# Layer 1's mixer weights split into two parts during layer 0's MLP, kept in device memory and reloaded through a ring of five places

## The chip, the cores and the metric

The kernel runs on one core of one Trainium2 chip. The metric is the device time of one execution in microseconds (us), median of several runs. The core's engines are named as the profile names them: PE (matrix products; PEld is its loading of the stationary operand), DVE (vector), ACT (scalar), POOL (GpSimd) and SP (which here only issues transfers). A transfer (DMA) is issued by an engine's queue; SP's and POOL's are used here.

## The reference

Two layers over a residual stream x of 1024 tokens x 1024 channels, in float32. Cut to what matters:

```python
for layer in range(2):
    h = rms_norm(x, norm_mix[layer])
    if layer % 2 == 0:
        y_mix, xq = rglru_group(h, w_in_a, ...)      # recurrent block
    else:
        y_mix, xq = fox_group(h, w_in_b, ...)        # forgetting attention, 8 heads of 64
    y_mem = memory_group(xq, mem, ..., w_mem_kv[layer], ...)   # cross-attention into 256 memory tokens
    x = x + concatenate([y_mix, y_mem]) @ w_out[layer]
    x = x + square(relu(rms_norm(x, norm_mlp[layer]) @ w_mlp_in[layer])) @ w_mlp_out[layer]
```

In layer 1 (fox_group) one projection `h @ w_in_b` gives queries, keys, values, forget logits and the memory queries; `memory_group` needs `rms_norm(mem) @ w_mem_kv[1]`.

## The kernel before, in words

**Split products.** Every large product is made from three matmuls. A float32 operand is split into a high part (`hi`, rounded to the format `float32r`) and a low part (`lo`, what is left), and the product is hi·hi + hi·lo + lo·hi (`t3`, line 394). For a weight tile, ACT copies the raw tile into `wh` and DVE (or POOL) subtracts that from the raw tile into `wl` (`_wpart`, L320 and L321). For a data tile ACT writes `r` (L501) and DVE the second `r` (L504), in `split_sb`.

**The plan of weights.** `run` first appends every weight tile that will be used, in order of use, to `self.plan`; `share` then decides, entry by entry, where its data comes from. A weight tile is 128 partitions x 1024 numbers (512 KB). Raw tiles are loaded by SP's queue into four raw buffers `wr0` to `wr3` (L316) and split into a ring of three places; a place is one pair `wh`, `wl`. `wnext` and `wpair` hand out the next one or two entries and call `_wsplit`, which prepares entries up to three ahead: an entry is prepared as soon as the place of the entry three before it is free. Layer 1's mixer uses several weights twice, once for each half (h = 0 and h = 1) of the tokens: on the first use the parts are split and also stored to device memory (`wsp`, L344, SP's queue), on the second they are loaded from there (entries `"ld"`, L336, POOL's queue). `TUNE["pb0"]` and its kin say which quarters of a split POOL does in place of DVE.

**Stages**, by time in the profile: layer 0's mixer up to about 315 us; layer 0's MLP up to 949 us; layer 1's keys and values of the memory (`kv`) from 949 to 972 us; then the memory queries (`xq_proj`), `fox_proj` of h = 0, `fox` (attention) woven with the output projection and with `fox_proj` of h = 1; layer 1's MLP from about 1535 us. In `kv`, `xq_proj` and `fox_proj` two weight entries are taken at a time (`wpair`): `kv` runs 2 token tiles through a pair, 24 matmuls of 256 columns each, the others run 4.

**Layer 0's MLP** has eight groups g; each has a first half `mlp_z` (products "b11", "b21", "t2", "t3", "t1", "t4", "b22" with w_mlp_in) and a second half `mlp_out` (the same seven names with w_mlp_out), 24 matmuls of 512 columns in each product. Seven split weights come from four raw tiles by additions on DVE (`_wunit`, L359 to L364). The second half's results are added to x in device memory by accumulating transfers (`send`, L1223, POOL's queue; `xspill` is x).

**Slots.** All working tiles of 128 x 512 share a pool of 86 places (`Slots`), named `f` (float32) or `r` (float32r). The place that was given back longest ago is taken next; its next writer waits until the last reader, a transfer perhaps, is done with it.

**What sets the order.** Each engine and each queue runs its own instructions in order. The framework orders them when the program is built, with a timeline of its own, so the order on the engines is fixed and can be read from the program.

Of the kernel before, what the change touches and what calls it, by code (L numbers as in the profile page):

```python
# [77 lines left out]
class Unit:  # L78
# [3 lines left out]
    def __init__(self, src, names, at):  # L82
        self.src, self.names, self.buf, self.dve = src, names, {}, False
# [43 lines left out]
def chain(*gs):  # L127
# [39 lines left out]
    "pa": (),  # L167
    "pb0": (1, 3),
    "pb1": (0, 1, 2, 3),
    "pb2": (3,),  # L170
    "pm0": (),
    "pm1": (1, 3),
# [3 lines left out]
class Builder:  # L176
# [4 lines left out]
    def __init__(self, ctx, tc, ins, out):  # L181
# [12 lines left out]
        self.wraw = [cst.tile([P, 1056], F32, name=f"wr{i}") for i in range(4)]  # L194
        self.ubuf = [self.wraw[3][:, i * 520:i * 520 + H + 3] for i in range(2)]
# [20 lines left out]
        self.pool_parts = TUNE["pa"]  # L216
# [11 lines left out]
        for _ in range(10):  # L228
            nc.tensor.matmul(warm[:, :P], lhsT=self.ones, rhs=self.ones, start=True, stop=True)

# [37 lines left out]

    def share(self):
        own, keep = {}, {}  # L270
        for j, e in enumerate(self.plan):
            if len(e) < 5 or e[3][0] not in ('wkb','wqb','wvb0','wvb1','wxqb','wout1m','wout1x'):
                continue
            k, full = e[3], self.ins[e[3][0]].shape[2]
            if k in own:
                if k not in keep:
                    keep[k] = [self.dr.tile([P, full], F32R, name=self.nm("wsp")) for _ in range(2)]
                self.plan[j] = (None, e[1], "ld", k, e[4])
            elif e[1] == full:
                own[k] = j  # L280
        k = ("wout1x", 3)
        keep[k] = [self.dr.tile([P, 1024], F32R, name=self.nm("wsp")) for _ in range(2)]
        self.own = {j: keep[k] for k, j in own.items() if k in keep}
        self.keep = keep
        self.raws, self.rawbuf, last = [], {}, [-1] * 4
        n, mod = 0, 3
        for j, e in enumerate(self.plan):
            if isinstance(e[2], Unit):
# [4 lines left out]
            for k, src, end in todo:  # L293
                b = n % mod
                n += 1
                self.raws.append((j, src, b, last[b]))
                last[b] = end
                if k is None:
                    self.rawbuf[j] = b
                else:  # L300
                    e[2].buf[k] = self.wraw[b][:, :1024]

    def _wbuf(self, i, bufs):
        return bufs[i % len(bufs)][:, :self.plan[i][1]]

    def _wrawbuf(self, i):
        return self.wraw[self.rawbuf[i]][:, :self.plan[i][1]] if i in self.rawbuf else None

    def _wraw(self, upto):
        while self.wrawn < len(self.raws):  # L310
            i, src, b, prev = self.raws[self.wrawn]
            if i >= upto or prev >= self.wload:
                break
            n = src.shape[1]
            for s in (slice(0, n // 2), slice(n // 2, n)) if self.wrawn == 0 else (slice(0, n),):
                self.nc.sync.dma_start(self.wraw[b][:, s], src[:, s])  # L316
# [6 lines left out]
    def _wsplit(self, upto):  # L323
        nc = self.nc
        while self.wload < min(len(self.plan), upto):
# [6 lines left out]
            hi, lo = (self._wbuf(i, b) for b in (self.whi, self.wlo))  # L332
# [15 lines left out]
    def _wunit(self, hi, lo, unit, what):  # L348
        V = self.nc.vector
        G = V if unit.dve else self.nc.gpsimd  # L350
        r = unit.buf
# [3 lines left out]
        for h in range(2):  # L355
# [3 lines left out]
            G.tensor_tensor(r["a11"][:, d], r["a11"][:, d], r["a21"][:, d], ALU.subtract)  # L359
            G.tensor_tensor(x, r["a22"][:, d], r["a11"][:, d], ALU.subtract)  # L360
# [1509 lines left out]
```

## Time and profile before

| what | value |
|---|---|
| median of 3 runs | 2077.35 us (2076.72 to 2081.33) |
| the profiled execution's own time | 2074.57 us |
| its span, first to last instruction | 2072.6 us |
| PE busy | 2045.0 us, 99% of the span |
| DVE, ACT, POOL busy | 1568.6, 1152.0, 456.8 us |
| transfers | 301.55 MB, mean 145 GB/s |

How to read the profile: "busy" is the time in which an engine ran an instruction other than one that waits, branches or issues a transfer for another engine. A row of the waits says who waited for whom, the sum in us, how often, and the longest. A row of the stages ("windows") gives, for a stretch of time, its length, then the busy time of each engine with the number of its instructions, then the granted clock of PE (1.00 is full), the mean busy share of the 16 transfer engines, and GB/s. A row of a transfer queue gives packets, MB, and the time that its packets took as a share of the 16 engines over the stretch. "Landing" is the time from the issue of a transfer to its end.

### The profile page before, as it was taken

The numbers are of one execution on the slowest core, as the hardware profiler recorded it, in microseconds if no ns is written. First come the engines' busy times: TensorE is split into PE (matmuls) and PEld (weight loads), VectorE is DVE, ScalarE is ACT, GpSimd is POOL, SyncE is SP. The second block draws the span as 40 slices with busy tenths as digits, with TensorE's granted clock in tenths as the row PEclk, the third lists the DMA queues.
The fourth block names the chain that finished last, engine by engine and source line by source line (L and its number), as shares of the span: only waits on it lengthen the run. The fifth ranks groups of instructions, "written<-read, shape, count | busy, mean of one in ns | idle before, by whom it ended". The sixth has DMA issues, their size and how long they took to land. (4 is left out here: it accounts for less than half of the span.)

```text
span 2072.6 us, 29660 instructions
## 1 busy us (share of the span) xinstructions
PE 2045.0 (99%) x10382; PEld 1707.0 (82%) x10382; DVE 1568.6 (76%) x2924; ACT 1152.0 (56%) x2172; POOL 456.8 (22%) x582
## 2 busy tenths in 40 slices
PE   9999999999999999999999999999999999999999
PEld 7998778888888888879998998777777888888887
DVE  8897699776776776788685779786886767758757
ACT  7856655554554554557554646575655445545543
POOL 1022210201202202205442423222021222022021
PEclk9999999999999999999999999999999999999999
DMA  8423361635635635638777438633355576265274
GB/s 295 150 95 118 102 208 62 132 82 112 133 82 112 133 78 116 144 112 254 254 248 266 153 111 300 212 132 127 126 117 144 136 159 122 67 138 117 68 182 122
DMA packets 122645, 301.55 MB, mean 145 GB/s; under 512 B 13760, under 2 KB 15872, under 8 KB 122496
## 3 DMA queue, kind: packets, MB, share of 16 engines
q1 hardware_dynamic: 80736, 211.50, 30.2%
q0 software_dynamic: 41760, 88.16, 22.7%
q8 instruction: 81, 1.33, 0.2%
q14 instruction: 68, 0.56, 0.1%
HBM read 190.46 MB, written 109.15 MB: 145 GB/s over the span
## 5 line engine op out<-in xcount | busy, mean ns | idle before, releaser
L1067 PE MATMUL pspt<-r,wh 128*128 128x512 f32 x1536 | 493.4, 397 | 1.8 <-ACT wh L320 1.6
L321 DVE TENSOR_TENSOR wl<-wr,wh 128x1024 fp32r<-128x1024 f32 (+2 forms) x354 | 338.5, 965 | 179.0 <-ACT wh L320 177.3
L320 ACT ACTIVATE wh<-wr 128x1024 fp32r<-128x1024 f32 (+3 forms) x403 | 303.3, 777 | 295.6 <-PE pss L1067 87.8
L1223 POOL DMA_DIRECT2D xspill<-f x232 | 203.0, 1087 | 858.9 <-DVE f L1083 821.4
L1067 PEld LDWEIGHTS pspt<-r,wh 128*128 128x128 f32 x1536 | 288.3, 188 | 73.1 <-ACT wh L320 2.4
L1067 PE MATMUL pss<-r,wh 128*128 128x512 f32 x1024 | 328.7, 396 | 0.8 <-DVE r L504 0.8
L1067 PE MATMUL pspt<-r,wl 128*128 128x512 f32 x768 | 304.5, 396 | 1.1 <-DVE wl L321 1.1
L1067 PE MATMUL pspj<-r,wh 128*128 128x512 f32 x832 | 272.8, 401 | 0.7 <-DVE r L496 0.7
L389 PE MATMUL pspj<-wh,r 128*128 128x256 f32 (+1 forms) x1280 | 244.1, 285 | 3.2 <-DMA wh<-wsp 1.4
L504 DVE TENSOR_TENSOR r<-f,r 128x512 fp32r<-128x512 f32 x282 | 188.9, 685 | 73.9 <-DMA xspill<-f 56.2
L1067 PEld LDWEIGHTS pss<-r,wh 128*128 128x128 f32 x1024 | 192.3, 188 | 48.7 <-DVE r L504 1.7
L501 ACT ACTIVATE r<-f 128x512 fp32r<-128x512 f32 x282 | 169.3, 625 | 79.5 <-DMA xspill<-f 24.7
L389 PEld LDWEIGHTS pspj<-wh,r 128*128 128x128 f32 x1280 | 201.5, 189 | 6.1 <-DMA wh<-wsp 1.9
L1067 PE MATMUL pss<-r,wl 128*128 128x512 f32 x512 | 202.5, 395 | 0.0
L1067 PEld LDWEIGHTS pspj<-r,wh 128*128 128x128 f32 x832 | 157.5, 190 | 39.2 <-DVE r L496 1.3
L389 PE MATMUL pspj<-wl,r 128*128 128x256 f32 (+1 forms) x640 | 182.3, 285 | 0.4 <-DVE wl L321 0.4
L1067 PEld LDWEIGHTS pspt<-r,wl 128*128 128x128 f32 x768 | 144.7, 188 | 36.5 <-DVE wl L321 1.5
L1067 PE MATMUL pspj<-r,wl 128*128 128x512 f32 x416 | 165.3, 398 | 0.0
L389 PE MATMUL pspj<-r,wh 128*128 128x512 f32 x480 | 157.5, 404 | 1.9 <-ACT r L493 0.5
L1088 ACT ACTIVATE f<-f 128x512 f32<-128x512 f32 x128 | 78.7, 625 | 102.9 <-DVE f L1087 100.7
L389 PEld LDWEIGHTS pspj<-wl,r 128*128 128x128 f32 x640 | 120.7, 189 | 1.6 <-DVE wl L321 0.6
L1067 PEld LDWEIGHTS pss<-r,wl 128*128 128x128 f32 x512 | 96.2, 188 | 23.5 <-issue 0.2
(302 smaller groups left out, 3564.2 us busy)
## 6 DMA issues: line engine op xcount, KB each, us to landing
wr<-in_w_dram SPq DMA_DIRECT2D x136, 512.0 KB, 4.0
xspill<-f POOLq DMA_DIRECT2D x232, 256.0 KB, 7.3
f<-xspill SPq DMA_DIRECT2D x88, 256.0 KB, 4.4
xspill<-f SPq DMA_DIRECT2D x56, 256.0 KB, 3.0
wsp<-wh SPq DMA_DIRECT2D x22, 512.0 KB, 5.9
wsp<-wl SPq DMA_DIRECT2D x22, 512.0 KB, 5.9
wh<-wsp POOLq DMA_DIRECT2D x21, 512.0 KB, 5.8
wl<-wsp POOLq DMA_DIRECT2D x21, 512.0 KB, 5.8
```

Of the source, the lines that this page charges most:

```text
L320: self.wact = self.nc.scalar.activation(hi, raw, AF.Copy)
L321: eng.tensor_tensor(lo, raw, hi.bitcast(F32), ALU.subtract)
L389: self.lastmm = self.nc.tensor.matmul(out, lhsT=a, rhs=b, start=(j == 0), stop=(j == n - 1))
L501: i = self.nc.scalar.activation(hi[:, :n], src, AF.Copy)
L504: self.nc.vector.tensor_tensor(lo[:, :n], src, hi[:, :n].bitcast(F32), ALU.subtract)
L1067: self.lastmm = self.nc.tensor.matmul(ps, lhsT=a, rhs=b, start=(start and c == 0 and j == 0), stop=(c == n - 1 and j == 2), skip_group_che ...
L1088: self.lastsq = self.nc.scalar.activation(f[:, n], f[:, n], AF.Square)
L1223: nc.gpsimd.dma_start(self.xs[2 * q + a, :, b * H:(b + 1) * H], f[:, n], accum_op=ALU.add)
```

## The change

The weights of layer 1's mixer (`LATE`, and the second half of `wkv`) are all made entries of the kind `"ld"`, first uses too. `share` lists them in `todo` as 66 pieces of up to 512 columns. During layer 0's MLP, at the start of most products from the second half of g = 0 on, `pre_tick` loads up to two pieces into slots (SP's queue, line 325 of the changed file), and three ticks later splits them with `split_sb` and stores both parts into `wsp` (POOL's queue, line 335: 132 stores of 256 KB). In the mixer all 55 uses are loads of 512 KB for each of the two parts (line 377, POOL's queue: 110 loads, where there were 46). The mixer no longer has any raw weights, so the four raw buffers become two more places: from the first `kv` entry to the last one of `fox_proj`, the ring has five. The table of POOL's quarters goes away.

The core of the diff:

```diff
+        self.wp = ctx.enter_context(tc.tile_pool(name="wp", bufs=1))
+        self.wide = [(-1, None)] * 4
...
     def share(self):
...
+            k = e[3]
+            if k[0] not in self.LATE and not (k[0] == "wkv" and k[1] >= 8):
+                continue
...
+            if k not in self.keep:
+                full = self.ins[k[0]].shape[2]
+                self.keep[k] = [self.dr.tile([P, full], F32R, name=self.nm("wsp")) for _ in range(2)]
+                n = -(-full // H)
+                self.todo += [(k, q * full // n, full // n) for q in range(n)]
+            self.plan[j] = (None, e[1], "ld", k, e[4])
+
+        rings = [(a, b) for a, b in zip(self.whi, self.wlo)]
+        wide = rings + [(0, 1), (2, 3)]
...
+            b = min(range(len(wide) if first <= j < end else len(rings)), key=lambda i: (used[i], i))
+            self.ring.append(wide[b])
+            self.prior.append(used[b])
+            used[b] = j
...
+    def pre_load(self, n):
+        for _ in range(min(n, len(self.todo))):
+            k, a, w = self.todo.pop(0)
+            f = self.F.get()
+            self.nc.sync.dma_start(f[:, :w], self.ins[k[0]][k[1]][:, a:a + w])
+            self.inload.append((self.ticks, k, a, w, f))
+
+    def pre_split(self):
+        self.ticks += 1
+        while self.inload and self.inload[0][0] <= self.ticks - 3:
+            _, k, a, w, f = self.inload.pop(0)
+            parts = self.split_sb(f[:, :w], w)
+            self.F.put(f)
+            for r, d in zip(parts, self.keep[k]):
+                self.nc.gpsimd.dma_start(d[:, a:a + w], r[:, :w])
+            self.R.put(*parts)
+
+    PRE = {"ot4": 2, "ob22": 2, "zb11": 2, "zb21": 2, "zt2": 2, "zt3": 1}
...
-    def _wsplit(self, upto):
-        while self.wload < min(len(self.plan), upto):
+    def _wsplit(self, at):
+        while self.wload < len(self.plan) and self.prior[self.wload] < at:
...
-                    self._wpart(hi[:, s], lo[:, s], raw[:, s], nc.gpsimd if q in self.pool_parts else nc.vector)
-                for b, d in zip((hi, lo), self.own.get(i, ())):
-                    nc.sync.dma_start(d.bitcast(F32), b.bitcast(F32))
+                    self._wpart(hi[:, s], lo[:, s], raw[:, s], nc.vector)
...
@@ mlp_z
+            if l == 0 and g:
+                self.pre_tick("z" + key)
             yield from self.product(banks, xp[key], start, done)
@@ mlp_out
+            if l == 0:
+                self.pre_tick("o" + key)
             yield from self.product(banks, hp[key], start, done)
```

How the instructions move, at two places, as the built programs have them. First POOL's queue in layer 0's MLP, at the sends of group g = 1 that follow its products "t4" and "b22"; `xspill` is x in device memory, `f` and `r` are slots, `wsp` the kept parts. Before:

```order
L1223 DMA xspill_101<-f37_504_4648 128x512
L1223 DMA xspill_101<-f42_505_4656 128x512
L1223 DMA xspill_101<-f84_506_4664 128x512
L1223 DMA xspill_101<-f39_520_4807 128x512
L1223 DMA xspill_101<-f0_507_4672 128x512
```

and now, the same sends:

```order
L335 DMA wsp_112<-r_567_5001 128x512
L1263 DMA xspill<-f_537_4755 128x512
L335 DMA wsp_113<-r_568_5002 128x512
L1263 DMA xspill<-f_538_4763 128x512
L335 DMA wsp_114<-r_573_5050 128x512
L1263 DMA xspill<-f_539_4771 128x512
L335 DMA wsp_116<-r_575_5056 128x512
L1263 DMA xspill<-f_557_4922 128x512
```

The stores of the parts stand between the sends, so a send is now issued behind stores that wait for a split on ACT or DVE.

Second, POOL's queue where layer 0's MLP ends and `kv` begins; `wl`, `wh` are the ring's places, and of the changed kernel `wr0_1` with `wr1_1` and `wr2_1` with `wr3_1` are the two more places. Before:

```order
L1223 DMA xspill_101<-f43_876_8182 128x512
L1223 DMA xspill_101<-f6_877_8190 128x512
L321 TENSOR_TENSOR wl0_76<-wr0_69,wh0_73 128x256 x2
L1223 DMA xspill_101<-f1_878_8198 128x512
L1223 DMA xspill_101<-f63_879_8206 128x512
L321 TENSOR_TENSOR wl1_77<-wr1_70,wh1_74 128x256 x2
L1223 DMA xspill_101<-f57_888_8325 128x512
L321 TENSOR_TENSOR wl2_78<-wr2_71,wh2_75 128x256
```

and now:

```order
L1263 DMA xspill_101<-f24_1088_8880 128x512
L377 DMA wh2_75<-wsp_10_110 128x1024
L377 DMA wl2_78<-wsp_11_111 128x1024
L1263 DMA xspill_101<-f27_1089_8889 128x512
L377 DMA wr1_1_8771<-wsp_13_113 128x1024
L377 DMA wr0_1_8770<-wsp_12_112 128x1024
L377 DMA wr3_1_8775<-wsp_15_115 128x1024
L377 DMA wr2_1_8774<-wsp_14_114 128x1024
L377 DMA wl0_76<-wsp_17_117 128x1024
```

POOL's subtractions are gone, and in their place POOL issues the loads of both parts, each when PE has let go of the place; the first two entries of `kv` (parts 2 to 5) are issued ahead of these rows, into the former raw buffers.

More of the change, by code (lines that the diff above doesn't have):

```diff
@@ L193, in __init__ @@
         self.F = Slots(up, F32, free, held)
-        self.wraw = [cst.tile([P, 1056], F32, name=f"wr{i}") for i in range(4)]
-        self.ubuf = [self.wraw[3][:, i * 520:i * 520 + H + 3] for i in range(2)]
+        self.wp = ctx.enter_context(tc.tile_pool(name="wp", bufs=1))
+        self.wide = [(-1, None)] * 4
+        self.ubuf = [self.wtile(3, 0)[:, i * 520:i * 520 + H + 3] for i in range(2)]
         self.whi = [cst.tile([P, 1056], F32R, name=f"wh{i}") for i in range(self.NRING)]
@@ L229, in __init__, with wtile @@
             nc.tensor.matmul(warm[:, :P], lhsT=self.ones, rhs=self.ones, start=True, stop=True)
+    def wtile(self, b, era):
+        if self.wide[b][0] != era:
+            assert self.wide[b][0] < era
+            dt = F32R if era == 1 else F32
+            self.wide[b] = era, self.wp.tile([P, 1056], dt, tag=f"wr{b}", bufs=1, name=f"wr{b}_{era}")
+        return self.wide[b][1]
     def nm(self, s):
@@ L267, in ent @@
         return (self.ins[name][i][:, a:a + n], n, parts, (name, i), a)
+    LATE = ("wkb", "wqb", "wvb0", "wvb1", "wxqb", "wout1m", "wout1x")
     def share(self):
-        own, keep = {}, {}
+        self.keep, self.todo, self.inload, self.ticks = {}, [], [], 0
+        first = end = None
         for j, e in enumerate(self.plan):
-            if len(e) < 5 or e[3][0] not in ('wkb','wqb','wvb0','wvb1','wxqb','wout1m','wout1x'):
+            if isinstance(e[2], Unit):
                 continue
[L274 to L285, printed above, removed]
+            k = e[3]
+            if k[0] not in self.LATE and not (k[0] == "wkv" and k[1] >= 8):
+                continue
+            if first is None:
+                first = j
+            if k[0] not in ("wout1m", "wout1x"):
+                end = j + 1
@@ new lines, in share @@
+            if k not in self.keep:
[6 more added lines that the diff above has]
+        wide = rings + [(0, 1), (2, 3)]
+        self.ring, self.prior, used = [], [], [-1] * len(wide)
@@ L286, in share @@
+        last, late = [-1] * 4, [-1] * 4
+        self.raws, self.rawbuf = [], {}
         n, mod = 0, 3
         for j, e in enumerate(self.plan):
+            b = min(range(len(wide) if first <= j < end else len(rings)), key=lambda i: (used[i], i))
+            self.ring.append(wide[b])
+            self.prior.append(used[b])
+            used[b] = j
+            if b >= len(rings):
+                late[2 * (b - len(rings))] = late[2 * (b - len(rings)) + 1] = j
             if isinstance(e[2], Unit):
@@ L292, in share @@
                 todo = [(None, e[0], j)] if e[0] is not None else []
-            for k, src, end in todo:
+            for k, src, stop in todo:
                 b = n % mod
                 n += 1
-                self.raws.append((j, src, b, last[b]))
-                last[b] = end
+                b = b, 0 if j < first else 2
+                self.raws.append((j, src, b, last[b[0]], late[b[0]]))
+                last[b[0]] = stop
                 if k is None:
@@ L300, in share, with pre_tick, _wbuf @@
                 else:
-                    e[2].buf[k] = self.wraw[b][:, :1024]
-    def _wbuf(self, i, bufs):
-        return bufs[i % len(bufs)][:, :self.plan[i][1]]
+                    e[2].buf[k] = b
+    def pre_load(self, n):
[14 more added lines that the diff above has]
+    PRE = {"ot4": 2, "ob22": 2, "zb11": 2, "zb21": 2, "zt2": 2, "zt3": 1}
+    def pre_tick(self, key):
+        self.pre_split()
+        self.pre_load(self.PRE.get(key, 0))
+    def _wbuf(self, i):
+        return [(self.wtile(b, 1) if isinstance(b, int) else b)[:, :self.plan[i][1]] for b in self.ring[i]]
     def _wrawbuf(self, i):
-        return self.wraw[self.rawbuf[i]][:, :self.plan[i][1]] if i in self.rawbuf else None
+        return self.wtile(*self.rawbuf[i])[:, :self.plan[i][1]] if i in self.rawbuf else None
     def _wraw(self, upto):
         while self.wrawn < len(self.raws):
-            i, src, b, prev = self.raws[self.wrawn]
-            if i >= upto or prev >= self.wload:
+            i, src, b, prev, late = self.raws[self.wrawn]
+            if i >= upto or prev >= self.wload or late >= self.wpos:
                 break
@@ L331, in _wsplit @@
             raw = self._wrawbuf(i)
-            hi, lo = (self._wbuf(i, b) for b in (self.whi, self.wlo))
+            hi, lo = self._wbuf(i)
             if parts == "ld":
@@ L349, in _wunit @@
         V = self.nc.vector
-        G = V if unit.dve else self.nc.gpsimd
-        r = unit.buf
+        r = {k: self.wtile(*b)[:, :1024] for k, b in unit.buf.items()}
         if what != "S2":
@@ L1054, in plan_mlp @@
         for g in range(8):
[L1055 to L1058 removed]
+            self.plan_unit("w1", 8 * l + g, Unit.ALL[2:] if g in parked + wait else Unit.ALL)
+            self.plan_unit("w2", 8 * l + g)
     def product(self, banks, parts, start, done=None):
```

38 lines of the change are left out of this document (10 added, 28 removed).

## The prediction

> **What bounds the kernel now.** I read the page's head first, then the stages, then the waits of PE. The head:
>
> ```profile
> PE 2045.0 (99%) x10382; PEld 1707.0 (82%) x10382; DVE 1568.6 (76%) x2924; ACT 1152.0 (56%) x2172; POOL 456.8 (22%) x582
> ```
>
> PE is the bound: of the span of 2072.6 us it is not busy for 27.6 us in all. The stages (length; PE, PEld, DVE, ACT, POOL; granted clock, transfer share, GB/s) say where: layer 0's MLP, the three stretches in which layer 1's weights are split, and three later ones.
>
> ```profile
> 330.00:930.00 600.00, 599.58 (x2572) 482.18 (x2572) 436.84 (x624) 303.04 (x469) 102.11 (x118) 1.00 0.49 109
> 950.00:1000.00 50.00, 50.00 (x424) 49.67 (x423) 41.16 (x94) 35.69 (x98) 22.85 (x27) 1.00 0.84 277
> 1000.00:1050.00 50.00, 49.22 (x403) 48.32 (x402) 36.05 (x92) 33.15 (x94) 26.66 (x35) 1.00 0.60 214
> 1050.00:1100.00 50.00, 49.00 (x344) 44.98 (x343) 37.88 (x100) 21.83 (x43) 15.24 (x16) 1.00 0.84 307
> ...
> 1300.00:1350.00 50.00, 47.50 (x230) 37.62 (x229) 34.59 (x84) 28.80 (x62) 13.77 (x21) 0.97 0.64 210
> 1350.00:1400.00 50.00, 48.10 (x252) 38.35 (x251) 42.07 (x110) 36.92 (x82) 14.22 (x22) 0.97 0.37 122
> ...
> 1450.00:1500.00 50.00, 48.17 (x216) 38.60 (x215) 42.88 (x73) 31.76 (x51) 1.41 (x4) 0.90 0.38 127
> ```
>
> The MLP loses 0.4 us of 600, the splitting stretches 0, 0.8 and 1.0 of 50 each. The last three lose 2.5, 1.9 and 1.8, and their clock costs more: 0.03, 0.03 and 0.10 of 50 us are 8 us of clock not granted. What PE waits for, from 940 to 1250 us:
>
> ```profile
> PE pso L1513 <- DVE f L1540: 1.7, 1, 1.7
> PE pspj L389 <- DVE f L948: 0.8, 2, 0.5
> PE pspj L389 <- DVE fl L1394: 0.8, 1, 0.8
> PE pspj L389 <- DMA wh<-wsp: 0.6, 2, 0.4
> PE pspj L389 <- DVE f L600: 0.5, 1, 0.5
> ```
>
> and from 1250 to 1540 us, the largest and the one that concerns the ring:
>
> ```profile
> PE pss L1481 <- DVE mn L1486: 3.7, 7, 0.8
> ...
> PE pspj L389 <- DMA wh<-wsp: 0.8, 1, 0.8
> ```
>
> No wait for a split stands among the first five; three small ones are for DVE emptying PSUM, behind which the splits stand in DVE's queue.
>
> **What is removed.** The splits of the mixer, by the same stages but for line 321 alone (DVE, POOL):
>
> ```profile
> 950.00:1000.00 50.00, 14.93 (x24) 21.98 (x25) 1.00 0.84 277
> 1000.00:1050.00 50.00, 7.38 (x12) 10.19 (x12) 1.00 0.60 214
> 1050.00:1100.00 50.00, 9.10 (x10) 4.97 (x6) 1.00 0.84 307
> ```
>
> That is 31.4 us of DVE and 37.1 us of POOL, much work and almost all hidden. What can come back is bounded by the waits: 0.8 + 0.8 + 0.5 for DVE and 0.6 for a reload, 2.7 us; the 1.7 us at L1513 belongs to the attention, where no split runs. I take 2.0 us, since half of DVE's other work stays. With five places in place of three, the late reload of 0.8 us goes too. Sum: -2.8 us; the ends are 0 and -5.2 (all five rows and the 0.8). The attention's own chain (L1486) isn't touched, so what is late next after a removed wait is the same PSUM emptying, sooner.
>
> **What is added to layer 0's MLP.** 66 pieces: 66 loads of 256 KB on SP, 66 splits on ACT and DVE, 132 stores on POOL. The rows of a split, of a send on POOL with its landing, and of the two kinds of transfer queue in this stage:
>
> ```profile
> L504 DVE TENSOR_TENSOR r<-f,r 128x512 fp32r<-128x512 f32 x282 | 188.9, 685 | 73.9 <-DMA xspill<-f 56.2
> L501 ACT ACTIVATE r<-f 128x512 fp32r<-128x512 f32 x282 | 169.3, 625 | 79.5 <-DMA xspill<-f 24.7
> L1223 POOL DMA_DIRECT2D xspill<-f x115: 842/873/1898, 371.8 to 939.4; - x115
> DMA to landing us min/median/max: 3.7/7.1/11.0
> q0 software_dynamic: 16128, 29.37, 30.9%
> q1 hardware_dynamic: 11179, 35.50, 18.1%
> ```
>
> DVE: 66 x 0.685 = 45.2, so 482 of 600 us. ACT: 66 x 0.625 = 41.3, so 344. POOL: at most 132 x 0.873 = 115, so 217. Transfers: the loads are 66 x 0.262 = 17.3 MB at q1's price (18.1% of 600 us for 35.50 MB, 3.06 us per MB), 53 us; the stores 34.6 MB between that price and q0's, which is for accumulating sends (30.9% of 600 for 29.37, 6.31 us per MB), 106 to 218 us. With 0.49 x 600 = 294 of now, 453 to 565 of 600 us. Nothing is full, but the transfers come near it, and three queues get longer: SP's weight loads (L316) stand behind piece loads that wait for a slot; POOL's sends stand behind stores that wait for a split; ACT and DVE wait for a slot until a store has landed. What hides that is seen in two waits of this stage:
>
> ```profile
> ACT wh L320 <- DMA wr<-in_w_dram: 37.6, 6, 12.2
> DVE r L504 <- DMA xspill<-f: 25.2, 5, 6.3
> ```
>
> ACT stood up to 12.2 us for a raw weight and DVE up to 6.3 us for a send, and PE lost nothing: the ring's three places and products of 5.6 us (24 matmuls at 600 us / 2572) cover that. A wait that meets the longest landing in place of the median is 11.0 - 7.1 = 3.9 us longer; in each of about six groups (4 pieces are handled in g = 0, 11 in each later g) that would be 23 us if none were hidden. Between 0 and 23 I take 1.5 us, near 0, because the rows show the cover; below nothing is excluded, as PE loses only 0.4 us here.
>
> **What is added to the mixer's reloads.** `kv` is where entries go fastest. Its first and its next stage's first matmul, the transfer load around it with its issues (from 930 to 975 us), and the loads of parts that the kernel has now (their issue on POOL, their landing, and queue q0 from 1095 to 1250 us, where it carries only them):
>
> ```profile
> 949.41 0.28 PE L389 MATMUL pspt<-wh,r 128*128 128x256 f32 x1
> ...
> 972.03 0.28 PE L389 MATMUL pspj<-wh,r 128*128 128x256 f32 x1
> ```
> ```profile
> 930.00:975.00 45.00, 45.00 (x299) 41.04 (x299) 40.50 (x74) 35.55 (x89) 24.76 (x29) 1.00 0.83 237
> ```
> ```profile
> q1 hardware_dynamic: 2908, 8.50, 54.5%
> ...
> wr<-in_wkv_dram SPq DMA_DIRECT2D x6, 512.0 KB, 6.1
> ...
> xspill<-f POOLq DMA_DIRECT2D x8, 256.0 KB, 7.7
> wr<-in_wxqb_dram SPq DMA_DIRECT2D x4, 512.0 KB, 4.3
> wsp<-wh SPq DMA_DIRECT2D x2, 512.0 KB, 6.0
> wsp<-wl SPq DMA_DIRECT2D x2, 512.0 KB, 5.2
> wr<-in_wkb_dram SPq DMA_DIRECT2D x1, 512.0 KB, 6.1
> ```
> ```profile
> L336 POOL DMA_DIRECT2D wh<-wsp x23: 527/535/680, 1097.8 to 1439.5; - x23
> ...
> DMA to landing us min/median/max: 3.7/5.8/9.4
> ```
> ```profile
> q0 software_dynamic: 4602, 16.83, 33.0%
> ```
>
> PE uses eight entries in 22.62 us, one in 2.83. An entry is now two parts, 1.05 MB, at 33.0% of 155 us for 16.83 MB (3.04 us per MB): 3.19 us of all transfer engines. So reloading is slower than use, and only the five places loaded ahead help. From 930 to 975 us: now 0.83 x 45 = 37.4 us; out go eleven raw loads and four stores, 15 x 0.524 = 7.9 MB at 2.89 us (54.5% of 45 for 8.50 MB), 22.7 us; in come nine entries (eight of `kv`, two of `xq_proj`, less one that is loaded before 930), 28.7 us. That makes 43.4 of 45: it just fits. Each entry's own deadline is as near. A pair lasts 22.62/4 = 5.65 us, its second entry is first read 12 of its 48 matmuls (1.4 us) into it, so a place let go at a pair's end must be full 7.1 us later: two issues on POOL of 0.54 and a median landing of 5.8 take 6.9. At the longest landing, 9.4, four such entries are 3.4 us late each, 13.6 us. The ends are 0 and 13.6; I take 1.5, near the median. The Trainium skill, page "DMA: Bandwidth & Descriptors", section "Anatomy of one DMA — SWDGE (gpsimd) path", fits a transfer as 2.0 us + bytes/436e3; by that 512 KB lands in 3.2 us, nothing is late, and the sum would be 1.5 us lower. The trace's 5.8 us says otherwise, and decides.
>
> Later pairs last 11.3 us (4 token tiles) and need 6.4 us of transfers: covered. But each of the 110 loads waits on POOL, in order, until PE lets its place go, and behind it on POOL stand the scaling of the memory queries, the normalising of the probabilities (L744, L1498) and the squares for the norm (L448), for which PE's transposes and DVE's norm wait. Now, for the 46 loads (945 to 1540 us):
>
> ```profile
> POOL wl L336 <- PE pspj L389: 37.1, 11, 13.1
> ```
>
> POOL stands up to 13.1 us there, and none of PE's waits shown above is for POOL. With five places a load asks for its place as early as before or earlier; I take 0, and keep as bounds 0 to 2 us, one wait of the largest kind seen at PE (1.7 us).
>
> **The sum.** -2.8 + 1.5 + 1.5 = +0.2 us on the profiled execution's 2074.57. The median of the runs is 2.8 us above that execution; I carry the change over: 2077.35 + 0.2, about 2077.5 us. A measurement of this kernel can tell about 0.2%, 4.2 us, from no change.
>
> **The rivals.** *Late reloads* (slower): the landing in `kv` grows past 6.0 us (7.1 less the issues), since eight sends share the engines there, and the four second entries come late. For: share 0.97 by the sum above. Against: half the entries are loaded ahead. Half to all of 13.6 us, in place of the 1.5: +5.5 to +12, 2083 to 2090 us.
>
> *The MLP's cover gives way* (slower): slot waits and the delayed SP loads exceed what the ring hides, 1 to 3.5 us in each of six groups: +6 to +21 in place of 1.5, 2082 to 2097 us. Against: waits of 12.2 and 6.3 us cost nothing.
>
> *More relief than the waits show* (faster): the lightened DVE and POOL remove the full 5.2 us, nothing is late, and half of the 8 us of clock not granted comes back as the attention shifts: -9.2, 2068 us; up to 2073. For: no gap is needed for such a shift. Against: no split but a few runs in those stretches. The page "TensorE: Matmul & The Clock Gate", section "What's actually happening", of the Trainium skill puts the half clock after an idle window of about 3.4 us; no PE wait here is longer than 1.7 us, so the trace doesn't show that trigger, and which gap sets it stays unknown.
>
> That the splits stay in the mixer is excluded: the program's order has only loads there.
>
> **How the numbers follow.** Forecast, within 0.2%: 0.42 (own range 2073.5 to 2081.5). Late reloads 0.24, the MLP's cover 0.13, more relief 0.21. So faster 0.21, same 0.42, slower 0.37. The range 2069.5 to 2089 leaves out about 0.07 of the relief below and 0.11 of the two slower cases above.
>
> **What would show it.** Right: PE busy over 599 of 600 us in the MLP with DVE near 480; no wait of PE for `wl` or `wh` in `kv` above 1 us; landings of the reloads near 6 us; DVE about 31 us lighter from 950 to 1100. Late reloads: waits PE L389 <- DMA of several us between 955 and 985. The cover gone: waits PE <- ACT or DVE in the MLP, once a group. Relief: PEclk 1.00 throughout. A span over 2085 or under 2070 would make the forecast wrong.

## The result and the profile after

The changed kernel takes 2111.68 us (median of 4 runs, 2109.17 to 2116.28) against 2077.03 us (4 runs, 2073.76 to 2081.33) beside it: a ratio of 1.0168, 95% interval 1.0142 to 1.0194. That is 34.6 us slower, and 22.7 us above the upper end of the forecast's range. The profiled execution took 2109.17 us with a span of 2107.4. Its head line:

```profile
PE 2055.7 (98%) x10382; PEld 1712.4 (81%) x10382; DVE 1569.8 (74%) x2935; ACT 1149.1 (55%) x2134; POOL 515.1 (24%) x729
```

PE has the same 10382 matmuls, but is not busy for 51.7 us of the span where it was 27.6 before, and its busy time is 10.7 us longer. To see where, both spans are cut at the same work, not at the same time: at the starts of the 1801st, 4401st, 5001st and 6501st matmul and of the last one. The four stretches are layer 0's MLP, `kv` with the attention's first steps, the next projections, and the rest. The columns are those of the prediction's stages. Before:

```profile
335.15:942.88 607.73, 607.31 (x2601) 488.22 (x2600) 443.57 (x636) 308.48 (x482) 107.10 (x124) 1.00 0.50 111
942.88:1017.08 74.20, 74.20 (x602) 72.59 (x601) 58.26 (x128) 50.92 (x135) 34.55 (x38) 1.00 0.82 272
1017.08:1218.70 201.62, 197.41 (x1502) 188.18 (x1501) 149.38 (x450) 114.30 (x294) 76.65 (x113) 1.00 0.59 206
1218.70:2067.64 848.94, 838.15 (x3884) 679.72 (x3882) 634.34 (x1099) 457.53 (x808) 176.17 (x227) 0.99 0.54 140
```

After:

```profile
335.07:973.84 638.77, 618.80 (x2601) 494.32 (x2600) 482.99 (x703) 340.31 (x548) 180.59 (x260) 0.98 0.72 185
973.84:1050.67 76.83, 75.09 (x602) 73.11 (x600) 36.13 (x94) 30.83 (x67) 23.74 (x38) 1.00 0.84 267
1050.67:1250.42 199.75, 197.21 (x1502) 188.64 (x1501) 138.29 (x432) 103.28 (x264) 76.65 (x123) 1.00 0.54 175
1250.42:2102.54 852.12, 837.75 (x3884) 679.49 (x3882) 628.34 (x1096) 453.39 (x801) 171.80 (x229) 0.99 0.53 137
```

The differences are +31.0, +2.6, -1.9 and +3.2 us, together about 35; the spans differ by 34.8. The MLP's 31.0 us split in two in its rows: PE's idle time grows from 0.4 to 20.0 us (19.6), and the same 2601 matmuls are busy for 11.5 us longer, at a granted clock of 0.98 instead of 1.00. No engine is full there: DVE 483 of 639 us, ACT 340, POOL 181, transfers 0.72. What PE waited for from 330 to 960 us is almost one row:

```profile
PE pspt L1103 <- ACT f L1114: 18.7, 6, 4.1
```

Six waits, one in each of the six bursts of eleven pieces (a burst runs from the second half of one group into the first half of the next), for the copy of a PSUM bank by ACT (L1114). ACT is busy half of the time, so the question is what held it. The fourth of the six, on ACT, from 659 to 670 us (the bracket is the idle time ahead of the row, and what ended it):

```profile
659.18 0.61 ACT L1114 ACTIVATE f<-pspt 128x512 f32<-128x512 f32 x1
668.27 0.63 ACT L539 ACTIVATE r<-f 128x512 fp32r<-128x512 f32 x1 [8.48 <-DMA f<-in_wkb_dram]
668.81 1.04 ACT L361 ACTIVATE wh<-wr 128x1024 fp32r<-128x1024 f32 x1
669.75 0.58 ACT L1114 ACTIVATE f<-pspt 128x512 f32<-128x512 f32 x1
```

The split of a piece (L539) stands between the two copies of one product. ACT is idle for 8.48 us until the piece's load has landed, and the second copy comes after it. PE, meanwhile, had gone on to the next product at 657.67 us and needed that bank again behind the matmul of 665.84 us:

```profile
657.67 0.63 PE L1103 MATMUL pspj<-r,wh 128*128 128x512 f32 x2
...
665.84 0.40 PE L1103 MATMUL pspt<-r,wl 128*128 128x512 f32 x1
670.38 1.22 PE L1103 MATMUL pspt<-r,wh 128*128 128x512 f32 x2 [4.15 <-ACT f L1114]
671.40 0.63 PE L1103 MATMUL pspt<-r,wl 128*128 128x512 f32 x1
```

After the gap the row of one matmul takes 0.63 us in place of 0.40; the granted clock there is 0.50, shown at the end. SP's queue is in order, and each piece load first waits for its slot. These four issues of 0.33 us are spread over 8 us; the piece that ACT waits for is the third, and it landed 8.0 us after its issue:

```profile
656.96 0.33 SPq L325 DMA_DIRECT2D f<-in_wkb_dram  x1
658.04 0.33 SPq L325 DMA_DIRECT2D f<-in_wqb_dram  x1
660.21 0.33 SPq L325 DMA_DIRECT2D f<-in_wkb_dram  x1
664.79 0.33 SPq L325 DMA_DIRECT2D f<-in_wqb_dram  x1
```

Over the whole MLP, SP's waits for a slot that an accumulating send still reads, and, from the view of L325, ACT's waits for the loads themselves:

```profile
SPq L325 <- DMA xspill<-f: 120.0, 34, 9.2
```
```profile
  ACT r L539: 74.2, 16
...
DMA to landing us min/median/max: 2.3/6.4/8.7
```

In the mixer, PE's waits from 970 to 1280 us show two late reloads of 0.9 and 0.8 us, which with 0.9 us of longer matmuls are `kv`'s 2.6 us; the row of the attention's own chain from 1280 to 1570 us is 6.6 us where it was 3.7:

```profile
PE pspt L427 <- DMA wr<-wsp: 0.9, 1, 0.9
PE pspt L427 <- DMA wl<-wsp: 0.8, 1, 0.8
```
```profile
PE pss L1519 <- DVE mn L1524: 6.6, 9, 2.7
```

### The profile page after: what moved, and what is told of

The parts are those of the page before. It is cut to its first block, busy times and chain, and to the rows that moved or that the text cites. A ratio compares the mean times of both kernels' runs of the same rounds, so it can differ in the third digit from the quotient of the medians.

```text
span 2107.4 us, 29999 instructions
## 1 busy us (share of the span) xinstructions
PE 2055.7 (98%) x10382; PEld 1712.4 (81%) x10382; DVE 1569.8 (74%) x2935; ACT 1149.1 (55%) x2134; POOL 515.1 (24%) x729
## 5 line engine op out<-in xcount | busy, mean ns | idle before, releaser
L1103 PE MATMUL pspt<-r,wh 128*128 128x512 f32 x1536 | 500.8, 403 | 21.8 <-ACT f L1114 18.7
L361 ACT ACTIVATE wh<-wr 128x1024 fp32r<-128x1024 f32 (+2 forms) x299 | 261.5, 887 | 238.2 <-PE pss L1103 68.4
L362 DVE TENSOR_TENSOR wl<-wr,wh 128x1024 fp32r<-128x1024 f32 (+2 forms) x299 | 300.8, 1014 | 120.9 <-ACT wh L361 119.7
L542 DVE TENSOR_TENSOR r<-f,r 128x512 fp32r<-128x512 f32 (+1 forms) x348 | 232.5, 685 | 118.5 <-ACT r L539 47.7
L539 ACT ACTIVATE r<-f 128x512 fp32r<-128x512 f32 (+1 forms) x348 | 208.9, 623 | 185.7 <-PE pso L1103 23.1
L1103 PE MATMUL pspj<-r,wh 128*128 128x512 f32 x832 | 271.7, 399 | 1.6 <-ACT f L1114 0.8
L1103 PEld LDWEIGHTS pspj<-r,wh 128*128 128x128 f32 x832 | 155.9, 189 | 41.3 <-ACT f L1114 2.6
L427 PE MATMUL pspj<-wh,r 128*128 128x256 f32 (+1 forms) x896 | 173.6, 285 | 0.2 <-ACT f L640 0.2
L427 PE MATMUL pspj<-r,wh 128*128 128x512 f32 x448 | 147.4, 403 | 2.8 <-DVE f L986 1.4
L427 PEld LDWEIGHTS pspj<-wh,r 128*128 128x128 f32 x896 | 141.6, 189 | 1.3 <-ACT f L640 0.4
L427 PE MATMUL pspj<-wl,r 128*128 128x256 f32 (+1 forms) x448 | 127.3, 285 | 0.4 <-DVE wl L362 0.4
L1119 DVE TENSOR_TENSOR f<-f,pspt 128x512 f32<-128x512 f32 x128 | 85.4, 683 | 33.5 <-PE pspt L1103 32.4
```

The costliest lines, as they stand in the source:

```text
L361: self.wact = self.nc.scalar.activation(hi, raw, AF.Copy)
L362: eng.tensor_tensor(lo, raw, hi.bitcast(F32), ALU.subtract)
L427: self.lastmm = self.nc.tensor.matmul(out, lhsT=a, rhs=b, start=(j == 0), stop=(j == n - 1))
L539: i = self.nc.scalar.activation(hi[:, :n], src, AF.Copy)
L542: self.nc.vector.tensor_tensor(lo[:, :n], src, hi[:, :n].bitcast(F32), ALU.subtract)
L1103: self.lastmm = self.nc.tensor.matmul(ps, lhsT=a, rhs=b, start=(start and c == 0 and j == 0), stop=(c == n - 1 and j == 2), skip_group_che ...
```

## The experiments

Theory: the loss is ACT standing at the split of a piece whose load is late, with PSUM copies queued behind it. Rivals: the added work and traffic as such (A), the mixer's reloads (B), and others named as they came. Each kernel was timed beside the kernel before, whose medians were 2076.75 to 2078.51 us.

**1. The split behind the copy.** Nothing changes but ACT's order:

```diff
-            parts = self.split_sb(f[:, :w], w)
+            parts = self.split_sb(f[:, :w], w, self.lastcopy)
...
-            self.nc.scalar.activation(f[:, :H], ps, AF.Copy)
+            self.lastcopy = self.nc.scalar.activation(f[:, :H], ps, AF.Copy)
```

> The changed kernel, but each piece's split on ACT is ordered behind the PSUM copy that was written before it in the program. Theory (the harm is that PSUM copies of the same product stand behind a split that waits for its load): ACT still waits for late loads, since the loads come as late as before, but the bank that PE needs is emptied first; the gap at the second product of a group goes or shrinks below 1 us, unless the next copy is caught: 2076 to 2092 us. Rival A (the added work and transfers as such) and rival B (the mixer's reloads): 2105 to 2115 us. Rival C (the loads' lateness reaches PE by another way than ACT's queue, through slots or DVE): 2100 to 2115 us.

Measured: 2082.63 us, ratio 1.0025 (1.0016 to 1.0035), inside the theory's range. All 66 loads, 66 splits and 132 stores are there, SP waits as before for slots (102.6 us), and of the 34.6 us 29 are gone. PE's waits in the MLP shrink to

```profile
PE pss L1103 <- DVE r L542: 3.3, 2, 2.9
```

This alone rules out A as the main cause, and B. One thing was not as expected: ACT no longer waits for a piece at all (the view of L325 names it no more; in the change it was 74.2 us), because behind the copy a split comes late enough for its load. So the run took away the wait ahead of the copy; it does not show a wait that stayed and did no harm.

**2. The split later, and earlier.** One number, `ticks - 3`, becomes 5 and 2:

```diff
-        while self.inload and self.inload[0][0] <= self.ticks - 3:
+        while self.inload and self.inload[0][0] <= self.ticks - 5:
```

> The changed kernel, but a piece is split five products after its load is issued, not three. Theory (ACT stands at a piece's split because the piece itself has not landed, copies of PSUM stand behind it, PE stops once a group, and the clock is halved after the gap): the six gaps of PE in layer 0's MLP (19.6 us, and 23.9 us at half clock) go, ACT's waits for piece loads fall from 73 us to under 10, and the time is 2076 to 2084 us. Rival A (the added work and transfers as such: 66 splits, 132 stores, 66 loads): they are all still there, so 2105 to 2115 us. Rival B (the mixer's 110 reloads): untouched, so 2105 to 2115 us.

> The changed kernel, but a piece is split two products after its load is issued, not three. Theory: each group's wait of ACT grows by up to one product (5.6 us), so gaps of 5 to 9 us in place of 3.3 in each of six groups, and more half clock behind them: 2130 to 2160 us. Rival A and rival B (work as such; the mixer's reloads): the work is the same, 2105 to 2115 us.

Measured: 2127.6 us (1.0232, 1.0209 to 1.0255) and 2099.85 us (1.0103, 1.0088 to 1.0118): both on the wrong side of what the theory said. With five products ACT hardly waits for a piece any more (2.5 us), and the time is worse. From 330 to 975 us in that run:

```profile
PE pspj L1103 <- ACT f L1114: 29.4, 12, 3.2
...
ACT f L1114 <- DMA xspill<-f: 26.5, 12, 3.8
...
ACT r L539 <- DMA wsp<-r: 14.5, 7, 4.9
```

Now the copies (L1114) and the splits wait for a slot of their own, whose send or store is under way. A piece that is held longer keeps its slot longer, which would leave fewer free; that this is the reason is argued, no run shows it. With two products ACT's waits for pieces fall too, to 7.8 us, where the theory had them grow; the splits now wait for slots of sends instead, and PE loses 11.7 us to copies behind them:

```profile
ACT r L539 <- DMA xspill<-f: 96.9, 28, 8.4
```

So the theory had to be widened: whatever makes ACT wait for a transfer ahead of a PSUM copy can cost PE, be it the piece's own load or a slot.

**3. The MLP's part alone, and in pieces.** The kernel before gets the loads, splits and stores of the change in layer 0's MLP; the mixer stays as it was and reads none of the stores. Then the stores are left out, then the splits too, and last the splits are put back but read a constant column:

```diff
+            if l == 0 and g:
+                self.pre_tick("z" + key)
...
+            parts = self.split_sb(f[:, :w], w)
...
-            parts = self.split_sb(f[:, :w], w)
+            parts = self.split_sb(self.par[:, 0:1].to_broadcast([P, w]), w)
```

> The kernel before, with the change's 66 loads, splits and 132 stores added to layer 0's MLP at the same places; nobody reads the stored parts, and the mixer splits its weights as before. Theory: the whole loss is there, in the MLP: 2077 + 32 = 2102 to 2115 us, with a gap of PE of 2.4 to 4.3 us in each of six groups. Rival B (the mixer's reloads carry a good part of the loss): 2077 to 2095 us.

> The kernel before with the change's 66 loads and splits added to layer 0's MLP, but without the 132 stores (nothing reads them). Theory (a piece's load gets a slot whose send is still under way, lands late, and ACT holds PSUM copies behind that piece's split): the loads ask for the same slots, so most of the loss stays, 2092 to 2107 us, with gaps of 2 to 4 us in most of the six groups. Rival D (the stores: their time on POOL ahead of the sends, their share of the transfer engines, the slots that they keep): 2076 to 2084 us.

> The kernel before with the change's 66 piece loads added to layer 0's MLP at the same places, and each slot given back three products later; nothing is split or stored. Theory: ACT has no split to stand at, so no gap of PE once a group: 2075 to 2082 us, though SP still waits for slots. Rival E (SP's weight loads behind piece loads that wait for a slot starve the ring of split weights): waits of ACT for a raw weight that reach PE, 2084 to 2100 us.

> As the run without stores, but the 66 splits read a column of constants that has been in place since the start; the 66 loads are still issued and nobody reads them. Theory (ACT stands at the split because the piece's load is late): the splits' own work stays on ACT and DVE, the wait goes: 2078 to 2085 us, as with the loads alone. Rival F (the split's work, or its own slots that wait for a send, does the harm): 2095 to 2125 us, as without stores.

Measured: 2106.91 us with everything (1.0134, 1.0117 to 1.0151); 2124.39 us without stores (1.0216, 1.0201 to 1.0232); 2081.3 us with the loads alone (1.0012, 1.0000 to 1.0024); 2077.38 us with loads and constant splits (1.0005, 0.9996 to 1.0014). The MLP's part carries the loss without any reload, so B falls. The stores do not carry it: without them it is worse than with them, worse also than the theory's 2092 to 2107. Its trace shows a likely reason. Leaving the stores out moved ACT's order, and the split that waits now stands ahead of both copies of the product, the first of which PE wants 2.8 us sooner than the second; PE's gap there is 5.50 us, where it was 4.15:

```profile
672.44 0.63 ACT L539 ACTIVATE r<-f 128x512 fp32r<-128x512 f32 x1 [7.82 <-DMA f<-in_wkb_dram]
```

The last of the four, 0.6 us below its range, has the same work on ACT and DVE, the same loads, and the same waits of SP for slots as the change (120.0 us there), but its splits need no load:

```profile
SPq L289 <- DMA xspill<-f: 122.9, 35, 10.2
```
```profile
338.22:945.95 607.73, 607.31 (x2601) 488.09 (x2600) 482.15 (x702) 340.36 (x547) 107.45 (x124) 1.00 0.59 139
```

607.73 us, to the hundredth what it was before the change, with DVE at 482 and ACT at 340 us. So the work and the loads as such cost nothing. The run does not part the wait from the order, though: splits that need no load stand elsewhere on ACT, and in five of the six bursts none is left between the two copies shown above. They still wait 26.9 us for slots of sends (3.6 us at most), and PE loses nothing by that, so a wait of ACT is not harmful by itself. The run with loads alone has one gap, and it is the same mechanism with another transfer: a raw weight behind piece loads on SP, for which ACT stood 15.59 us, the copies of three banks behind it, and PE 2.75 us for the third:

```profile
642.65 1.06 ACT L356 ACTIVATE wh<-wr 128x1024 fp32r<-128x1024 f32 x1 [15.59 <-DMA wr<-in_w_dram]
...
645.09 0.60 ACT L1114 ACTIVATE f<-pspj 128x512 f32<-128x512 f32 x1
```
```profile
645.74 0.50 PE L1103 MATMUL pspj<-r,wh 128*128 128x512 f32 x1 [2.75 <-ACT f L1114]
```

**4. Why the loads are late.** Two slots fewer; slots of sends and stores given out last; and no sends in layer 0's MLP at all:

```diff
-    NU = 86
+    NU = 84
```
```diff
-            self.free_.append((t_ids.pop(id(t)), given[0], stream[0]))
+            self.free_.append((t_ids.pop(id(t)), given[0] + later, stream[0]))
...
-            self.F.put(f)
+            self.F.put(f, later=16)
...
-            self.R.put(*parts)
+            self.R.put(*parts, later=16)
```
```diff
-            nc.gpsimd.dma_start(self.xs[2 * q + a, :, b * H:(b + 1) * H], f[:, n], accum_op=ALU.add)
+            if l:
+                nc.gpsimd.dma_start(self.xs[2 * q + a, :, b * H:(b + 1) * H], f[:, n], accum_op=ALU.add)
```

> The changed kernel with 84 slots in place of 86. Theory in its wider form (slots are scarce; whoever asks gets one whose send is younger by two slots): loads of pieces come later and more of ACT's own copies wait for a slot, gaps longer by 0.5 to 2 us or more of them in each group: 2115 to 2135 us. Rival G (the load's own time, not its slot, is what is late): 2107 to 2115 us, as the change.

> The changed kernel, but a slot given back by a send or a store counts as given back 16 later, so that whoever asks gets slots without a transfer under way first. Theory (the loads are late because their slots' sends have not landed): SP's waits of piece loads for sends fall from 120 us to under 50, ACT's for pieces from 73 us to under 25, gaps mostly gone: 2078 to 2096 us. Rival G (the transfer itself and SP's queue make them late): ACT still stands 60 to 80 us for pieces, 2104 to 2115 us.

> The changed kernel without the accumulating sends of layer 0's MLP (its result is left out of the residual, so that what the later stages compute is not the reference's); loads, splits and stores of pieces stay, and splits still stand between PSUM copies on ACT. Theory (a piece's load waits on SP for a slot whose send is under way): SP's waits of L325 for sends go, ACT stands under 15 us for pieces, no gap of over 2 us in the MLP: 2068 to 2084 us. Rival G (the load's own transfer or SP's order makes it late): ACT stands 50 us or more for pieces, gaps as in the change: 2098 to 2115 us.

Measured: 2100.96 us (1.0115, 1.0100 to 1.0131), 2105.02 us (1.0134, 1.0118 to 1.0149) and 2077.43 us (0.9999, 0.9989 to 1.0008). The first two missed. With 84 slots the time fell by 10.7 us where it should have risen: pieces held ACT for 26.2 us, its own copies for

```profile
ACT f L1114 <- DMA xspill<-f: 32.0, 20, 3.7
```

and the ten gaps of PE were at most 1.8 us, after none of which the clock dropped. Giving out sends' slots last did not lower SP's waits, as it was meant to, but raised them to 159.4 us, so it tests nothing. ACT stood 33.9 us for pieces there, so rival G's sign did not come either, though its time did. Both edits also move instructions on ACT, and neither run parts that from the age of a slot. In the third, SP's waits for sends are gone, ACT's for pieces down to

```profile
  ACT r L539: 10.4, 4
...
DMA to landing us min/median/max: 2.3/3.5/7.1
```

and the MLP has no gap (607.74 us). ACT's order moved here as well, but a split still stands between the two copies of the product. So the sends make the loads late, by the slots that they keep and by the transfer time that they take (a median landing of 6.4 us became 3.5; in the run that kept the sends and left out the stores it was 5.7); this run does not part the two.

**5. Can the order be mended?** All start from experiment 1. Loads moved away from the sends' end, then only thinned out, then with sends' slots given out last as well:

```diff
-    PRE = {"ot4": 2, "ob22": 2, "zb11": 2, "zb21": 2, "zt2": 2, "zt3": 1}
+    PRE = {"zb11": 2, "zb21": 3, "zt2": 3, "zt3": 3}
+        while self.inload and self.inload[0][0] <= self.ticks - 2:
...
+    PRE = {"ob22": 2, "zb11": 3, "zb21": 3, "zt2": 3}
...
+    PRE = {"ob22": 2, "zb11": 2, "zb21": 2, "zt2": 2, "zt3": 2}
...
+    PRE = {"ot4": 1, "ob22": 2, "zb11": 2, "zb21": 2, "zt2": 2, "zt3": 1}
```

> The changed kernel with the split on ACT ordered behind the copy before it (as in the run that moved only that), and the loads issued later in a group, when its sends have had more time to land: 2 at zb11, 3 each at zb21, zt2 and zt3, split two products later. Theory: SP waits for slots under 40 us in place of 120, ACT for piece loads and slots under 10, no gap in the MLP: 2073 to 2080 us, the mixer's part within 3 us of before. Rival A (work as such still costs some us): 2081 to 2088 us.

> As the run with later loads, but 2 at ob22, 3 each at zb11, zb21 and zt2, split three products later, as in the change. Theory: SP's waits for slots fall less (to 40 to 80 us), the splits come at products with fewer free slots, so a gap or two may be left: 2075 to 2086 us. Rival A (work as such): as the other, 2081 to 2088 us.

> The run with the split behind the copy before it, and without loads at ot4, whose slots are the youngest: 2 each at ob22, zb11, zb21, zt2 and zt3, split three products later. Theory: SP's waits for slots fall below 102 us and the one gap of 3.1 us near 690 us goes: 2074 to 2081 us. Rival H (what is gained at the loads is lost at the splits, which come one product later, where fewer slots are free, as in the two runs with later loads): 2090 to 2120 us.

> The run with the split behind the copy before it, and one load in place of two at ot4. Theory: the one gap near 690 us goes and splits stay where they were: 2075 to 2081 us. Rival H: the order of ACT shifts and a gap comes back in each group: 2090 to 2120 us.

> The run with the split behind the copy before it and one load at ot4, with the slots of sends and stores given out last as well. Theory: the MLP stays without a gap, SP's waits for sends fall; what is left is the mixer's: 2079 to 2086 us. Rival H (other orders of ACT bring gaps back): 2090 to 2115 us.

Measured, in this order: 2117.09 us (1.0189, 1.0175 to 1.0203), 2119.69 us (1.0203, 1.0189 to 1.0218), 2097.29 us (1.0098, 1.0084 to 1.0112), 2085.57 us (1.0039, 1.0026 to 1.0052) and 2092.08 us (1.0073, 1.0059 to 1.0087). All five miss the theory's range on the slow side, by 4.6 us (the fourth) to 37 us (the first). Where rival H was named, it was right for the third and the last. For the last, though, PE's gaps are waits for DVE (9.3 us in six), not for ACT. In the first, ACT no longer stands for a single piece, but a split waits for a slot, with a copy behind it:

```profile
460.62 0.63 ACT L539 ACTIVATE r<-f 128x512 fp32r<-128x512 f32 x1 [4.21 <-DMA xspill<-f]
461.16 0.58 ACT L1114 ACTIVATE f<-pss 128x512 f32<-128x512 f32 x1
```

PE loses 21.1 us in six waits for such copies. The fourth has an MLP almost without a wait, 609.84 us, and loses its time in `kv` (945 to 1025 us), as the first two do beside their gaps:

```profile
PE pspt L427 <- DMA wr<-wsp: 2.8, 1, 2.8
```

**6. Without the reloads in `kv`.** The eight entries of `kv` are split at their use as before the change, two of four parts on POOL; once on the order of the fourth kernel above with nine pieces a group, once on experiment 1 itself:

```diff
-            if k[0] not in self.LATE and not (k[0] == "wkv" and k[1] >= 8):
+            if k[0] not in self.LATE:
...
-                    self._wpart(hi[:, s], lo[:, s], raw[:, s], nc.vector)
+                    self._wpart(hi[:, s], lo[:, s], raw[:, s], nc.gpsimd if k_pool and q in (1, 3) else nc.vector)
```

> The run with the split behind the copy before it and one load at ot4, and the eight entries of kv are split at their use as before the change (two of four parts on POOL), so that 50 pieces are left in the MLP, nine a group; the other entries are reloaded through the ring of five. Theory (the reloads in kv come late, about 3 us): the gap of 3 us in kv goes, 2076 to 2082 us. Rival I (the rest is the mixer's clock or its other reloads): 2083 to 2087 us.

> The run with the split behind the copy before it (loads and splits at the change's own places), with the eight entries of kv split at their use as before the change: 50 pieces in the MLP, the other entries reloaded through the ring of five. Theory: the MLP loses 0 to 6 us as in that run (2082.6), kv's 2.6 us go, and the 1.7 us that the stretch behind kv gains stay: 2075 to 2082 us. Rival I (what is left is the later mixer's clock): 2082 to 2087 us.

Measured: 2085.4 us (1.0045, 1.0031 to 1.0058), 3.4 us over the theory's range and inside rival I's, and 2077.74 us (1.0003, 0.9994 to 1.0012), inside the theory's. In both, `kv` is back at 73.99 us, so its reloads are what it lost. The first kernel had four gaps of ACT's order in the MLP again (616.22 us) and a slower clock later. The second, by the same stretches as above:

```profile
335.22:944.22 609.00, 608.58 (x2601) 487.60 (x2600) 472.53 (x687) 335.60 (x532) 159.83 (x224) 1.00 0.69 173
944.22:1018.21 73.99, 73.99 (x602) 72.71 (x600) 47.09 (x110) 40.69 (x99) 30.39 (x42) 1.00 0.73 221
1018.21:1218.27 200.06, 197.26 (x1503) 188.49 (x1502) 137.88 (x432) 103.03 (x264) 76.28 (x123) 1.00 0.53 175
1218.27:2071.81 853.54, 838.99 (x3884) 681.06 (x3882) 627.59 (x1096) 452.71 (x801) 172.26 (x229) 0.99 0.54 137
```

With ACT's order mended and `kv` undone, the whole loss is gone. The MLP has sixteen pieces fewer here, so its 609.00 us (613.40 in experiment 1) are not owed to the order alone. Nothing is won against the kernel before either: no version was faster than it.

## Why the prediction was wrong

The step that failed is the term of +1.5 us for layer 0's MLP, "near 0, because the rows show the cover". It measured 31.0 us. The forecast took two waits that cost nothing, ACT's 12.2 us for a raw weight and DVE's 6.3 us for a send, as the depth of a cover that any wait would find. But a wait has the cover of the bank whose copy is queued behind it: the time until PE wants that bank. The rows of before show that the 12.2 us wait had PSUM copies behind it too, and how little was left:

```profile
872.32 1.06 ACT L320 ACTIVATE wh<-wr 128x1024 fp32r<-128x1024 f32 x1 [12.16 <-DMA wr<-in_w_dram]
...
874.76 0.60 ACT L1078 ACTIVATE f<-pspj 128x512 f32<-128x512 f32 x1
```
```profile
875.93 0.63 PE L1067 MATMUL pspj<-r,wh 128*128 128x512 f32 x2
```

The copy ended at 875.36 us and PE wanted the bank at 875.93, 0.6 us later: the cover was 12.7 us, and all but used up. The run with loads alone shows it again from the other side: 15.59 us at the same place cost 2.75 us, a cover of 12.8. DVE's 6.3 us had reads of PSUM right behind it as well (L1083, at 623.16 us). Behind the split of a piece stands the second copy of a product whose bank was full at 657.67 us, when PE went on to the next product, and wanted again at 666.24 us (665.84 + 0.40), 8.6 us later. Of these 8.6 us ACT's other rows, the split, a raw split and the copy itself take about half; ACT's idle 8.48 us made the copy 4.15 us late, so the cover there was 4.3 us, not 12.

Second, the list of queues in that step lacked one. It named ACT and DVE waiting for a slot, POOL's sends behind stores, and SP's weight loads behind piece loads. It did not name ACT waiting for the landing of the piece load itself, which adds up what it had named: SP's slot waits and then a landing. That is 74.2 us in 16 waits; with the split behind the copy they are gone and the stage is back from 638.8 to 613.4 us. The price of a group's delay was taken from one landing that is longer than the median (11.0 - 7.1 = 3.9 us); SP's in-order queue alone spread four issues over 8 us.

Third, the bound of 23 us counted waits and not the clock. The six waits were 18.7 us, inside that bound; the half clock behind five of the six gaps added 11.5 us. The forecast had said of the clock that which gap sets it stays unknown, and then left it out of the sum.

The rival with the least chance, that the MLP's cover gives way, was the right mechanism but for the thing that gives way (it named the ring; it was a PSUM bank), and its sign in the profile, PE's waits for ACT once a group, is what came. Its price of 1 to 3.5 us a group was 3.1 us for the waits; with the clock it is 5.2 us.

The other steps:

- The work added to the MLP: forecast 45.2 us of DVE, 41.3 of ACT and at most 115 of POOL; over the same matmuls it was 39.4, 31.8 and 73.5. (Six of the 66 pieces are 352 columns wide, so six loads and twelve stores are of 176 KB, not 256.) Transfers grew by 156 us (0.72 of 638.8 less 0.50 of 607.7), at the lower end of 159 to 271. The work was counted a little high; it just wasn't the cost.
- The mixer's relief, -2.8 us: -1.9 us in the stretch behind `kv`, and -1.6 in the last kernel of experiment 6. DVE is 33.2 us lighter in the two stretches (22.1 and 11.1), forecast 31.4.
- The reloads in `kv`, +1.5 us with ends 0 and 13.6: +2.6 us, up to 4.3 us in the fourth kernel of experiment 5 (78.49 against 74.20) and 4.5 in its first (78.74), and -0.2 us where `kv` isn't reloaded. The mechanism and the size were right: transfers at 0.84, late by up to 2.8 us. The rival's full price of 5.5 us and more was not reached.
- POOL's waits, 0: PE waited for POOL once in the whole run, 0.2 us.
- The rest of the mixer, 0: +3.2 us here. Of kernels with the old mixer its row is 848.9 us (before), 850.4 (the MLP's part alone), 849.7 (the constant splits) and 852.6 (the loads alone); with the new one 850.4 (experiment 1), 848.1 (the split later), 848.8 (the third of experiment 5) and 853.5 (the last of experiment 6). The two kinds overlap, so these 3.2 us stay unexplained and need not be the change's.

Two rules of the Trainium skill were weighed in the prediction. On the landing, "DMA: Bandwidth & Descriptors", "Anatomy of one DMA — SWDGE (gpsimd) path", gave 3.2 us for 512 KB; the 110 reloads here landed in 6.0 us at the median and 12.8 at most, which is longer than the rule says, as it was before the change. On the clock, "TensorE: Matmul & The Clock Gate", "What's actually happening", puts the half clock after an idle window of about 3.4 us. Now the trace has gaps of that size, and it agrees only roughly: shorter gaps were followed by half clock too, and one about as long was not (see below); the runs decide.

## What to carry to other kernels

Before work is added to an engine that also frees PSUM, list for each added instruction what it can wait for and which copy stands behind it; the cover is the time until PE wants that bank, not the longest wait seen elsewhere to be harmless. Where buffers come from one shared list, holding or asking for one at another moment moves the waits of everybody; here four of five attempts to place loads and splits better moved the gaps, while tying the split behind the copy had closed all but one at once. Put a price on the clock behind PE's waits as well: here 19.6 us of idle time, in gaps of 2.3 to 4.2 us, cost 31.0 us, about one and a half times as much.

## What was not expected of the hardware

The clock behind a gap. In the changed kernel, around the gap of 4.15 us that ends at 670.38 us and around that of 2.28 us that ends at 836.80 us (length; PE, PEld, DVE, ACT, POOL; granted clock; the last two columns, on transfers, are not used here):

```profile
665.00:670.00 5.00, 1.24 (x6) 0.66 (x4) 0.81 (x2) 1.73 (x3) 1.69 (x4) 0.83 1.16 294
670.00:675.00 5.00, 4.62 (x11) 3.65 (x12) 3.61 (x6) 2.21 (x5) 1.21 (x3) 0.50 1.20 386
675.00:680.00 5.00, 5.00 (x23) 4.01 (x22) 5.00 (x9) 5.00 (x9) 2.96 (x6) 0.98 0.95 294
```
```profile
835.00:840.00 5.00, 3.20 (x14) 2.62 (x15) 3.21 (x4) 2.25 (x4) 1.06 (x2) 1.00 1.17 341
840.00:845.00 5.00, 5.00 (x23) 4.04 (x22) 4.84 (x8) 4.97 (x10) 1.91 (x4) 1.00 1.21 401
```

At the long gap the clock is at half for 2 x (0.17 + 0.50 + 0.02) x 5 = 6.9 us, about 2 us of them still within the gap; the rest costs half its length. The short gap is followed by none. Of the six gaps, of 3.30, 3.24, 2.64, 4.15, 3.06 and 2.28 us, all but the last were followed by it. The length of a gap does not decide alone. In the run with the MLP's part alone, a gap of 3.2 us that ends at 589.4 us was followed by full clock, and one of 2.1 us that ends at 843.1 us by less:

```profile
590.00:595.00 5.00, 5.00 (x23) 4.05 (x22) 3.79 (x7) 3.02 (x5) 1.89 (x4) 1.00 1.19 392
845.00:850.00 5.00, 5.00 (x18) 3.95 (x17) 3.76 (x7) 4.29 (x8) 1.59 (x3) 0.76 1.19 399
```

What else decides was not tested. In the run with 84 slots, whose gaps are under 2 us, the clock stayed at 1.00 through the MLP. That is much of why its ten small gaps (12.0 us of waits in all) cost so much less than the six larger ones (18.7).

Loads that ran beside the accumulating sends landed late: the piece loads took 6.4 us at the median with the sends and 3.5 us without them, with the same loads and stores in the stage.
